# First two head projections of a hybrid backbone block: 128-column idle products, latent-token products of the second weight pair for both heads ahead of the context products, and the context squares' adds behind the latent tiles

## The chip, the cores and the metric

The program runs on one core of a Trainium2 chip. The metric is device time in microseconds (us) of one execution. The engines are PE (matrix products), DVE (vector), ACT (scalar), POOL and SP; nearly all loads are issued by SP's queue, in its program order. A block of 128 x 512 elements is written 128x512 here, 128 being the partitions.

## The reference

One layer of a generator block over 512 latent tokens and 256 context tokens, width D = 2048. Only its beginning matters here:

```python
mod = (c_act @ w_mod + b_mod)[:, None, :]            # c_act = silu(c)
mod_c = (cc_act @ w_mod + b_mod)[None, None, :]      # cc_act = silu(c_ctx)
sh1, sc1, gt1, sh2, sc2, gt2 = jnp.split(mod, 6, axis=-1)
...
h = rmsnorm(x, g_norm1) * (1 + sc1) + sh1            # latent tokens
hc = rmsnorm(ctx, g_norm1) * (1 + csc1) + csh1       # context tokens
lat_in, lat_gates = project_heads(h, w_in, ...)
ctx_in, ctx_gates = project_heads(hc, w_in, ...)
```

`rmsnorm` divides a token by the root of its mean square over the 2048 channels. `project_heads` multiplies by `w_in` (queries, keys and values of four GLA heads and four mLSTM heads). Scans over the tokens, an output projection and an MLP with a convolution follow; the change leaves them alone.

## The kernel before, in words

All matrix data are float32. A product of two float32 tiles is made of three products of parts: each operand is cut into a high part `hi` (a cast on ACT, line 110) and a low part `lo` (a subtraction on DVE, line 112), and `mm3` adds hi*hi, hi*lo and lo*hi (line 117 for all of them). A product written `fp32` (the modulation, the idle products, the sums of squares) goes through PE uncut and shows as two records in the trace.

The 2048 channels are 16 blocks of 128, taken as eight pairs `kp` = 0 to 7. `project_first` projects the first two heads, head 1 and head 0, pair by pair. A pair needs:

- Modulation. `mod_load(region, n)` loads four quarters (512 KB each) of the columns of `w_mod` for pair n; region 1 is the scale, region 0 the shift. `mod_rows` multiplies them by the activated c (tile `cact`) into the bank `ps_m`, and ACT copies the sums out (tile `rows_m`, line 299). `mod_cols` turns them into columns on PE (line 122), and DVE makes `scol` (scale) or `shcol` (shift) of them (lines 310 to 323).
- Tokens. `modulate` multiplies the latent block `xl` by `scol` and by the reciprocal root `rl` on DVE (line 808), and the context block `xc` by `scol` and `rc` (line 810). ACT then adds `shcol` and writes the high part (`hTh` for latent, `hch` for context, line 801), and DVE the low part (`hTl`, `hcl`, line 802).
- Weights. One 512 KB load `raw_h` for each head, cut into `hi_h` and `lo_h`.
- Products, in six groups g: queries and keys on latent tokens (0, 1), values on latent tokens (2, 3) and keys with values on context tokens (4, 5). Head 1's go through two turning PSUM banks (`early_group`, tile `a1`), and DVE adds each to a sum in SBUF (line 448, tile `e`). Head 0's add up in six banks of their own (`project_chunk`, tile `a0`). The trace calls both `a`.

Pair 0 is projected before any root is known, on tokens without root and shift (`bare`). Meanwhile `stream_rstd` squares the 16 latent blocks on ACT (line 770) and adds them on DVE (line 105, tile `sq_l`); one fp32 product with ones (`ss_l`) sums over partitions, and `mean_rsqrt` (lines 184 to 189) makes `rl`. The same is done for the eight context loads (`sq_c`, `ss_c`, `rc`). With a root known, pair 0's results are scaled after the fact: `scale_first` multiplies those with tokens in the free dimension by `rl` on DVE (line 102), `columns` makes columns `rcol` of the root (line 496, tile `diag`), and ACT scales the others by them (line 507). `shifted` adds the shift to `xl` for a later stage (line 823).

`idle(n)` issues n fp32 products on `cact` whose result nobody reads. `silu_rows` makes rows of the activated c, which POOL writes to DRAM (`crow_d`) and `last_rows` reads back spread over all partitions (two loads of 512 KB in SBUF), for the part of the modulation that DVE computes in later pairs.

What sets the order: within `project_first` every PE instruction is pinned to the order of the code (`tc.keep_in_program_order`). The other engines' orders are made by a scheduler, which puts work under `tc.high_priority()` first and obeys `tc.issue_after(ins)` (and `behind`, a list of them): an instruction is placed behind `ins` in the order, without a wait. At run time each engine goes through its list in order, and an instruction that waits for a semaphore holds up all behind it. A load waits for a free buffer: `raw_h` and every fourth modulation quarter share four (pool `wraw`), the other quarters seven (`mraw`).

Of the kernel before, what the change touches and what calls it, by code (L numbers as in the profile page):

```python
# [88 lines left out]
def block_kernel(ctx: ExitStack, tc: tile.TileContext, a: dict, out: bass.AP):  # L89
# [374 lines left out]
    def silu_rows():  # L464

        cr = [tmp.tile([2 * KT, P], F32, name=f"cr{i}", tag="rows") for i in range(2)]
        nc.sync.dma_start(cr[0], a["c_row"])
        S.activation(cr[1], cr[0], AF.Exp, scale=-1.0)
        V.tensor_scalar(out=cr[1], in0=cr[1], scalar1=1.0, scalar2=None, op0=ALU.add)
        V.reciprocal(out=cr[1], in_=cr[1])  # L470
        mul(cr[1], cr[0], cr[1])
        nc.gpsimd.dma_start(crow_d, cr[1])

    def idle(n):

        ps = psb("idle")
        for _ in range(n):
            mm(ps, flat(cact[:, 0:4, :]), flat(cact), start=True, stop=True)
# [20 lines left out]
    def scale_first(banks, sums, stream):  # L499
# [4 lines left out]
        for o in (sums, banks):  # L504
            for j in range(TJ) if stream == "x" else range(TJ, TJ + CJ):
                part = o[2 + j // 2][:, j % 2, :] if stream == "x" else o[j]
                S.activation(part, part, AF.Copy, scale=rcol[:, j : j + 1])
# [43 lines left out]
    def project_first():  # L551
# [12 lines left out]
        rows = mod_rows(1, 0, first_mod, lambda: idle(1))  # L564
        idle(1)
# [6 lines left out]
        idle(3)  # L572
# [5 lines left out]
        w1 = load_split(a["w_heads"][1, 1], "h1_1", by=OFF)  # L578
        for j in range(1, KT // 2):
            nc.sync.dma_start(xcp[j], a["ctxT"][j])  # L580
        w0_raw = load_raw(a["w_heads"][0, 1], "h0_1")
        stream_rstd(xl, rl, "l", T, bared)
        for g in range(2, 5):
            project_chunk(0, *w0, banks[g], g, 0, 1)
        rows = mod_rows(1, 1, raws[1])
        project_chunk(0, *w0, banks[5], 5, 0, 1)
        mod_cols(1, 1, *rows)
        rows = mod_rows(0, 1, raws[0])
        idle(1)
        mod_cols(0, 1, *rows)  # L590
        with tc.high_priority():
            modulate(1, "x")
            columns(range(TJ))
            scale_first(banks, sums, "x")
        for r in (1, 0):
            raws[r] = mod_load(r, 2)
        idle(3)
# [11 lines left out]
        for kp in range(1, KP):  # L609
            if kp == 1:  # L610
                silu_rows()
            for g in range(6):
                if g == 5 and 1 < kp < KP - 2:
                    rows = mod_rows(0, kp + 1, raws[0])
                if kp == 1 and g == 2:
                    with tc.high_priority():
                        stream_rstd([x.rearrange("p a b -> p (a b)") for x in xcp], rc, "c", TC)
                        modulate(1, "c")
                        columns(range(TJ, TJ + CJ))
                        scale_first(banks, sums, "c")  # L620
# [10 lines left out]
                if g == 2:  # L631
                    with tc.issue_after(ins):
                        if kp == 1:
                            with tc.high_priority():
                                w0 = split_new(w0_raw, "h0_1", (2, 512), by=OFF)
                        else:
                            w0 = load_split(a["w_heads"][0, kp], f"h0_{kp}", by=OFF)
# [4 lines left out]
                    if 1 < kp < KP - 3:  # L642
# [7 lines left out]
            if kp > 1 and kp + 1 < KP:  # L650
# [10 lines left out]
            for g in range(6):  # L661
                if g == 3 and 1 < kp < KP - 3:
                    rows = mod_rows(1, kp + 2, raws[1])
                if kp == 1 and g in (2, 4):
                    r = 2 - g // 2
                    rows = mod_rows(r, 2, raws[r])
# [18 lines left out]
                if g == 3 and 1 < kp < KP - 3:  # L685
# [1236 lines left out]
```

## Time and profile before

| what | value |
|---|---|
| median of 3 runs | 2393.97 us (2393.84 to 2395.94) |
| the profiled execution | 2394.47 us |
| its span in the trace | 2392.8 us |
| PE busy | 2360.2 us, 99% of the span |
| mean granted PE clock | 0.997 |
| first product of pair 0, of pair 1, of pair 2 | 18.48, 47.22, 78.19 us |

The profile is of one execution. Times on the timeline count from the start of the span. A timeline row gives the start, the duration, the engine, the line, the operation, output and inputs, the count of records merged, and in brackets the idle time of the engine before it and what ended that. Records of PE overlap: a 128x512 product that takes 0.39 us is followed by the next after 0.23 us.

### The profile page before, as it was taken

To read this page: it belongs to the slowest core of one execution; us is meant where nothing else is said; L and a number is where in the kernel's file an instruction comes from. 1 tells how busy PE (TensorE), PEld (TensorE's weight loads), DVE (VectorE), ACT (ScalarE), POOL (GpSimd) and SP (SyncE) were. 2 spreads that over 40 slices of the span, in tenths; PEclk is the share of its full clock that TensorE was granted. 3 is DMA by queue.
4 is the path that set the end of the run, shared out by engine and by line. 5 is a ranking of instruction groups with operands and counts; after the bars stand their busy time and mean duration, and the time that the engine had idled before them with its cause. 6 is when DMAs were issued, how large, how long until landed. Compare 5 with 4: busy or idle time off the path is not lost.

```text
span 2392.8 us, 38575 instructions
## 1 busy us (share of the span) xinstructions
PE 2360.2 (99%) x15310; PEld 2117.2 (88%) x15310; DVE 1811.7 (76%) x2924; ACT 1044.8 (44%) x1573; POOL 184.2 (8%) x236
## 2 busy tenths in 40 slices
PE   8999999999999999999999999999999999999998
PEld 4788899899998888888999999999999999999997
DVE  5777866654546676768998787878787878787886
ACT  5234543322233232327554444545454444444445
POOL 0000000000000000010011111111111111101022
PEclk9999999999999999999999999999999999999999
DMA  8871111234445879862374646464646464646464
GB/s 337 312 278 53 47 54 45 66 111 133 126 160 182 264 269 309 281 219 74 112 180 125 158 124 158 124 158 123 157 125 156 126 155 126 156 125 158 131 182 137
DMA packets 121703, 377.84 MB, mean 158 GB/s; under 512 B 14200, under 2 KB 15218, under 8 KB 121522
## 3 DMA queue, kind: packets, MB, share of 16 engines
q1 hardware_dynamic: 94066, 319.77, 40.7%
q0 software_dynamic: 27024, 54.82, 12.9%
q8 instruction: 120, 1.97, 0.3%
q10 hardware_dynamic: 432, 0.79, 0.1%
q14 instruction: 61, 0.50, 0.1%
HBM read 324.84 MB, written 50.48 MB: 157 GB/s over the span
## 4 chain that ended last, share of the span: by engine, by line
PE 93%; DVE 4%; ACT 2%; issue 1%; DMA 0%; DVEq 0%; ACTq 0%
PE dn L117 19%; PE uv L117 17%; PE ug L117 17%; PE a L117 17%; PE ga L117 7%; PE wo L117 7%; PE po L117 2%; PE ps_m L117 1%; PE sl L117 1%; PE st L117 1%; PE cst L117 1%; DVE ex L99 1%; PE idle L117 0%; DVE lo_h L112 0%; DVE e L448 0%
## 5 line engine op out<-in xcount | busy, mean ns | idle before, releaser
L117 PE MATMUL dn<-gh,hi_d 128*128 128x512 f32 x672 | 261.6, 389 | 0.0
L117 PE MATMUL dn<-gl,hi_d 128*128 128x512 f32 x672 | 261.5, 389 | 0.0
L117 PE MATMUL dn<-gh,lo_d 128*128 128x512 f32 x672 | 261.5, 389 | 0.0
L1639 DVE SCALAR_TENSOR_TENSOR cv<-pads,cwt,cv 128x512 f32<-128x512 f32 x344 | 240.8, 748 | 0.6
L1707 POOL DMA_DIRECT2D x2d<-st x160 | 139.6, 926 | 1096.3 <-ACT st L1706 1049.1
L112 DVE TENSOR_TENSOR lo_buv<-sum_uv,hi_buv 128x1024 fp32r<-128x1024 f32 x80 | 98.0, 1225 | 82.2 <-ACT hi_buv L110 80.2
L340 DVE SCALAR_TENSOR_TENSOR raw_m<-raw_m,crow 128x1024 f32<-128x1024 f32 x128 | 154.6, 1229 | 1.8 <-DMA raw_m<-in_w_mod 1.8
L117 PE MATMUL a<-hi_h,hTh 128*128 128x256 f32 x512 | 151.4, 296 | 1.4 <-ACT e L460 0.8
L117 PEld LDWEIGHTS dn<-gh,lo_d 128*128 128x128 f32 x672 | 126.1, 188 | 26.3
L117 PEld LDWEIGHTS dn<-gh,hi_d 128*128 128x128 f32 x672 | 126.1, 188 | 26.0 <-DVE u_ug L99 0.3
L117 PEld LDWEIGHTS dn<-gl,hi_d 128*128 128x128 f32 x672 | 126.1, 188 | 25.9
L117 PE MATMUL a<-lo_h,hTh 128*128 128x256 f32 x512 | 143.1, 279 | 0.0
L117 PE MATMUL a<-hi_h,hTl 128*128 128x256 f32 x512 | 142.9, 279 | 0.0
L112 DVE TENSOR_TENSOR lo_d<-raw_d,hi_d 128x1024 fp32r<-128x1024 f32 (+1 forms) x86 | 102.9, 1197 | 40.6 <-ACT hi_d L110 40.6
L110 ACT CAST hi_d<-raw_d 128x1024 fp32r<-128x1024 f32 (+1 forms) x86 | 88.7, 1032 | 101.8 <-PE dn L117 38.0
L117 PE MATMUL uv<-bqh,lo_auv 128*128 128x256 f32 x480 | 132.9, 277 | 0.0
L117 PE MATMUL uv<-bql,hi_auv 128*128 128x256 f32 x480 | 132.9, 277 | 0.0
L117 PE MATMUL ug<-bqh,lo_aug 128*128 128x256 f32 x480 | 132.8, 277 | 0.0
L117 PE MATMUL uv<-bqh,hi_auv 128*128 128x256 f32 x480 | 132.8, 277 | 0.0
L117 PE MATMUL ug<-bqh,hi_aug 128*128 128x256 f32 x480 | 132.8, 277 | 0.0
L117 PE MATMUL ug<-bql,hi_aug 128*128 128x256 f32 x480 | 132.8, 277 | 0.0
L117 PE MATMUL ug<-bth,hi_bug 128*128 128x256 f32 x480 | 132.6, 276 | 0.0
(482 smaller groups left out, 7282.4 us busy)
## 6 DMA issues: line engine op xcount, KB each, us to landing
raw_m<-in_w_mod SPq DMA_DIRECT2D x184, 512.0 KB, 5.3
raw_d<-in_w_down SPq DMA_DIRECT2D x82, 512.0 KB, 3.3
raw_ug<-in_w_up SPq DMA_DIRECT2D x80, 512.0 KB, 3.5
raw_uv<-in_w_up SPq DMA_DIRECT2D x80, 512.0 KB, 4.3
x2d<-st POOLq DMA_DIRECT2D x160, 256.0 KB, 5.4
raw_h<-in_w_heads SPq DMA_DIRECT2D x64, 512.0 KB, 3.6
raw_ga<-in_w_gates SPq DMA_DIRECT2D x32, 512.0 KB, 4.2
raw_wo<-in_w_out SPq DMA_DIRECT2D x32, 512.0 KB, 4.7
```

Of the source, the lines that this page charges most:

```text
L99: V.tensor_tensor(out=o, in0=x, in1=y, op=ALU.subtract)
L110: cast[0] = S.copy(hi, x).ins
L112: return V.tensor_tensor(out=lo, in0=x, in1=hi.bitcast(F32), op=ALU.subtract).ins
L117: ins = PE.matmul(*args, **kw)
L340: V.scalar_tensor_tensor(out=x, in0=x, scalar=1.0, in1=crow[0], op0=ALU.mult, op1=ALU.mult, accum_out=mtot[:, at : at + 1])
L1639: V.scalar_tensor_tensor(out=t3, in0=src, scalar=w, in1=t3, op0=ALU.mult, op1=ALU.add)
L1707: nc.gpsimd.dma_start(x2d[k], t, accum_op=ALU.add)
```

## The change

- `idle` multiplies 128 columns instead of 512, and there are 34 idle products instead of 15: 4 at the start as before, 2 instead of 1 between the quarters of the first modulation and around its columns, 8 instead of 3 ahead of pair 0, 2 at each of the columns of pair 1, and 10 instead of 3 ahead of pair 1.
- Pair 0 of head 0: its six groups all stand ahead of the latent root's product `ss_l`; before, groups 2 to 5 stood behind it.
- Pair 1 is taken out of the loop over `kp` and written out. On PE: groups 0 to 3 of head 1, groups 0 to 2 of head 0, then the context root `ss_c`, the scale's modulation of pair 2, group 3 of head 0, the shift's modulation of pair 2, then the context groups 4 and 5 of head 1 and of head 0. Before, `ss_c` stood behind group 1 of head 1, and each head's six groups stood together.
- `stream_rstd` of the context gets `(ins, ins)`: all its DVE adds, and its first two squares on ACT, are placed behind the last latent low part of pair 1 (`hTl`). `scale_first` gets two such lists: head 1's scaling stands behind the cast of its weights for pair 1, head 0's behind the cast of its own.
- Head 0's weights of pair 1 are cut right after pair 1's tokens are modulated. `silu_rows` (its tiles now under a tag of their own), `last_rows` and the load of the remaining constants move with the code, and so do the loads of later pairs in SP's queue. From pair 2 on the loop is as before, without its cases for pair 1; the counts of all real products are the same.

```diff
@@ -463,7 +463,7 @@
 
     def silu_rows():
 
-        cr = [tmp.tile([2 * KT, P], F32, name=f"cr{i}", tag="rows") for i in range(2)]
+        cr = [tmp.tile([2 * KT, P], F32, name=f"cr{i}", tag="cr") for i in range(2)]
         nc.sync.dma_start(cr[0], a["c_row"])
         S.activation(cr[1], cr[0], AF.Exp, scale=-1.0)
         V.tensor_scalar(out=cr[1], in0=cr[1], scalar1=1.0, scalar2=None, op0=ALU.add)
@@ -473,9 +473,9 @@
 
     def idle(n):
 
-        ps = psb("idle")
+        ps = psb("idle", (P, P))
         for _ in range(n):
-            mm(ps, flat(cact[:, 0:4, :]), flat(cact), start=True, stop=True)
+            mm(ps, flat(cact[:, 0:4, :]), flat(cact[:, 0:4, :]), start=True, stop=True)
 
     def bare(n, streams):
 
@@ -496,7 +496,7 @@
             V.scalar_tensor_tensor(out=junk, in0=rstd[:, P * j : P * j + P], scalar=1.0, in1=ident, op0=ALU.mult,
                                    op1=ALU.mult, accum_out=rcol[:, j : j + 1])
 
-    def scale_first(banks, sums, stream):
+    def scale_first(banks, sums, stream, queue=(), late=()):
 
         if stream == "x":
             for o in (*sums[0:2], *banks[0:2]):
@@ -504,7 +504,8 @@
         for o in (sums, banks):
             for j in range(TJ) if stream == "x" else range(TJ, TJ + CJ):
                 part = o[2 + j // 2][:, j % 2, :] if stream == "x" else o[j]
-                S.activation(part, part, AF.Copy, scale=rcol[:, j : j + 1])
+                with behind(late if o is banks else queue):
+                    S.activation(part, part, AF.Copy, scale=rcol[:, j : j + 1])
 
     first_bias = {}
 
@@ -561,40 +562,69 @@
         load_tokens(range(2, KT))
         raws = {r: mod_load(r, 1) for r in (1, 0)}
         idle(4)
-        rows = mod_rows(1, 0, first_mod, lambda: idle(1))
-        idle(1)
+        rows = mod_rows(1, 0, first_mod, lambda: idle(2))
+        idle(2)
         ins = mod_cols(1, 0, *rows)
         with tc.high_priority():
             w1 = split_new(w1_raw, "h1_0", (2, 512), by=OFF, after=(ins,))
             bared = bare(0, "x")
             w0 = split_new(w0_raw, "h0_0", (2, 512), by=OFF, after=bared[1:])
             bare(0, "c")
-        idle(3)
+        idle(8)
         early_pair(w1, sums)
         for g in range(2, 6):
             early_group(0, g, w1, sums)
         for g in range(2):
             project_chunk(0, *w0, banks[g], g, 0, 1)
         w1 = load_split(a["w_heads"][1, 1], "h1_1", by=OFF)
+        w1_cast = cast[0]
         for j in range(1, KT // 2):
             nc.sync.dma_start(xcp[j], a["ctxT"][j])
         w0_raw = load_raw(a["w_heads"][0, 1], "h0_1")
+        for g in range(2, 6):
+            project_chunk(0, *w0, banks[g], g, 0, 1)
         stream_rstd(xl, rl, "l", T, bared)
-        for g in range(2, 5):
-            project_chunk(0, *w0, banks[g], g, 0, 1)
         rows = mod_rows(1, 1, raws[1])
-        project_chunk(0, *w0, banks[5], 5, 0, 1)
+        idle(2)
         mod_cols(1, 1, *rows)
         rows = mod_rows(0, 1, raws[0])
-        idle(1)
+        idle(2)
         mod_cols(0, 1, *rows)
         with tc.high_priority():
-            modulate(1, "x")
+            ins = modulate(1, "x")
             columns(range(TJ))
-            scale_first(banks, sums, "x")
+            w0 = split_new(w0_raw, "h0_1", (2, 512), by=OFF)
+            scale_first(banks, sums, "x", (w1_cast,), (cast[0],))
+        silu_rows()
         for r in (1, 0):
             raws[r] = mod_load(r, 2)
-        idle(3)
+        idle(10)
+        for g in range(4):
+            early_group(1, g, w1, sums)
+        for g in range(3):
+            project_chunk(1, *w0, banks[g], g)
+        with tc.high_priority():
+            stream_rstd([x.rearrange("p a b -> p (a b)") for x in xcp], rc, "c", TC, (ins, ins))
+            modulate(1, "c")
+            columns(range(TJ, TJ + CJ))
+            scale_first(banks, sums, "c")
+        rows = mod_rows(1, 2, raws[1])
+        project_chunk(1, *w0, banks[3], 3)
+        mod_cols(1, 2, *rows)
+        rows = mod_rows(0, 2, raws[0])
+        early_group(1, 4, w1, sums)
+        mod_cols(0, 2, *rows)
+        ins = early_group(1, 5, w1, sums)
+        with tc.high_priority():
+            modulate(2, "xc")
+        w1 = load_split(a["w_heads"][1, 2], "h1_2", by=OFF)
+        raws[1] = mod_load(1, 3)
+        for g in range(4, 6):
+            project_chunk(1, *w0, banks[g], g)
+        with tc.issue_after(ins):
+            last_rows(0)
+            shifted(1)
+        nc.sync.dma_start(cst[:, 0:C_ID], a["consts"][:, 0:C_ID])
         loads = {(2, 0): (0, 1), (2, 1): (0, 0), (3, 0): (1, 1), (3, 1): (1, 0)}
         turns = {(2, 1): (0, 1), (3, 0): (0, 0), (4, 0): (1, 1), (4, 1): (1, 0)}
         lasts = {}
@@ -606,18 +636,10 @@
             if what == (1, 0) and g == 4:
                 last_end()
 
-        for kp in range(1, KP):
-            if kp == 1:
-                silu_rows()
+        for kp in range(2, KP):
             for g in range(6):
-                if g == 5 and 1 < kp < KP - 2:
+                if g == 5 and kp < KP - 2:
                     rows = mod_rows(0, kp + 1, raws[0])
-                if kp == 1 and g == 2:
-                    with tc.high_priority():
-                        stream_rstd([x.rearrange("p a b -> p (a b)") for x in xcp], rc, "c", TC)
-                        modulate(1, "c")
-                        columns(range(TJ, TJ + CJ))
-                        scale_first(banks, sums, "c")
                 if kp == 2 and g == 2:
                     rows = mod_rows(1, 3, raws[1])
...
@@ -659,30 +677,20 @@
                 with tc.issue_after(ins):
                     shift_first(1, sums)
             for g in range(6):
-                if g == 3 and 1 < kp < KP - 3:
+                if g == 3 and kp < KP - 3:
                     rows = mod_rows(1, kp + 2, raws[1])
-                if kp == 1 and g in (2, 4):
-                    r = 2 - g // 2
-                    rows = mod_rows(r, 2, raws[r])
                 if kp == KP - 3 and g == 1:
                     rows = mod_rows(0, 0, raws[2])
                 project_chunk(kp, *w0, banks[g], g)
                 with tc.issue_after(ins):
                     last_step(kp, 1, g)
-                if kp == 1 and g in (2, 4):
-                    mod_cols(2 - g // 2, 2, *rows)
                 if g == 2 and kp + 1 < KP:
                     w1 = load_split(a["w_heads"][1, kp + 1], f"h1_{kp + 1}", by=OFF)
-                    if kp == 1:
-                        raws[1] = mod_load(1, 3)
-                        with tc.issue_after(ins):
-                            last_rows(0)
-                        nc.sync.dma_start(cst[:, 0:C_ID], a["consts"][:, 0:C_ID])
-                    elif kp + 2 < KP - 1:
+                    if kp + 2 < KP - 1:
                         raws[0] = mod_load(0, kp + 2)
                     if (kp, 1) in loads:
                         lasts[loads[kp, 1]] = last_load(*loads[kp, 1])
-                if g == 3 and 1 < kp < KP - 3:
+                if g == 3 and kp < KP - 3:
                     mod_cols(1, kp + 2, *rows)
                 if kp == KP - 3 and g == 2:
...
```

Around the latent root, PE's order. `a_1_171` to `a_5_175` are head 0's banks of groups 1 to 5 (the last number is a buffer's), `ps_m_1` is the modulation of pair 1. Before:

```order
L117 MATMUL a_1_171<-hTh_259,lo_h_0_264 128x512
L117 MATMUL ss_l<-sq_l,cst 128x512
L117 MATMUL a_2_172<-hi_h_0_263,hTh_255 128x256
...
L117 MATMUL a_2_172<-hi_h_0_263,hTl_260 128x256
...
L117 MATMUL a_4_174<-hi_h_0_263,hch_267 128x384
...
L117 MATMUL a_4_174<-hi_h_0_263,hcl_272 128x384
L117 MATMUL ps_m_1_457<-raw_m_1_0_198,cact 32x256 x4
...
L117 MATMUL a_5_175<-hi_h_0_263,hch_267 128x384
...
L122 MATMUL ps_m_1_457<-cst,rows_m_1_474 128x128 x2
```

After:

```order
L117 MATMUL a_1_171<-hTh_263,lo_h_0_268 128x512
L117 MATMUL a_2_172<-hi_h_0_267,hTh_259 128x256
...
L117 MATMUL a_3_173<-hi_h_0_267,hTh_259 128x256
...
L117 MATMUL a_4_174<-hi_h_0_267,hch_271 128x384
...
L117 MATMUL a_5_175<-hi_h_0_267,hcl_276 128x384
L117 MATMUL ss_l<-sq_l,cst 128x512
L117 MATMUL ps_m_1_472<-raw_m_1_0_198,cact 32x256 x4
...
L117 MATMUL idle<-cact 128x128 x2
L122 MATMUL ps_m_1_472<-cst,rows_m_1_489 128x128 x2
```

Groups 2 to 5 of head 0 stand ahead of `ss_l`, and nothing but idle products stands between the modulation's sums and its columns.

Around the context root, PE's order. `a_1_0` to `a_1_5` are head 1's groups of pair 1, `ss_c` the context squares' sum, `ps_m_2` the modulation of pair 2, `a_2_0` pair 2's first group. Before:

```order
L117 MATMUL a_1_0_570<-hTh_514,hi_h_1_357 128x512
...
L117 MATMUL a_1_1_578<-hTh_514,hi_h_1_357 128x512
...
L117 MATMUL ss_c<-sq_c,cst 128x256 x2
L117 MATMUL a_1_2_638<-hi_h_1_357,hTh_514 128x256
...
L117 MATMUL a_1_4_670<-hi_h_1_357,hch_622 128x384
...
L117 MATMUL a_0_170<-hTh_514,hi_h_1_652 128x512
...
L117 MATMUL ps_m_2_700<-raw_m_2_0_542,cact 32x256 x4
...
L117 MATMUL a_3_173<-hi_h_1_652,hTh_514 128x256
...
L117 MATMUL ps_m_2_766<-raw_m_2_0_550,cact 32x256 x4
...
L117 MATMUL a_5_175<-hi_h_1_652,hch_622 128x384
...
L117 MATMUL a_2_0_821<-hTh_805,hi_h_2_738 128x512
```

After:

```order
L117 MATMUL a_1_0_594<-hTh_527,hi_h_1_366 128x512
...
L117 MATMUL a_1_1_602<-hTh_527,hi_h_1_366 128x512
...
L117 MATMUL a_1_3_624<-hi_h_1_366,hTh_527 128x256
...
L117 MATMUL a_0_170<-hTh_527,hi_h_1_543 128x512
...
L117 MATMUL a_2_172<-hi_h_1_543,hTh_527 128x256
...
L117 MATMUL ss_c<-sq_c,cst 128x256 x2
L117 MATMUL ps_m_2_714<-raw_m_2_0_567,cact 32x256 x4
...
L117 MATMUL a_3_173<-hi_h_1_543,hTh_527 128x256
...
L117 MATMUL ps_m_2_750<-raw_m_2_0_575,cact 32x256 x4
...
L117 MATMUL a_1_4_769<-hi_h_1_366,hch_698 128x384
...
L117 MATMUL a_1_5_781<-hi_h_1_366,hch_698 128x384
...
L117 MATMUL a_2_0_841<-hTh_793,hi_h_2_811 128x512
```

`ss_c` moved behind five more groups, and the context groups moved behind both modulations of pair 2.

Between the latent root and pair 1, DVE's order. `rstd` is the root, `e_0`, `e_1`, `a_0_170` and `a_1_171` the results of pair 0 that are multiplied by it, `xl_130` and `xl_131` pair 1's latent blocks. Before:

```order
L189 SCALAR_TENSOR_TENSOR rstd<-scr_l,rstd 128x512
L102 TENSOR_TENSOR e_0_293<-e_0_293,rstd 128x512
L102 TENSOR_TENSOR e_1_295<-e_1_295,rstd 128x512
L102 TENSOR_TENSOR a_0_170<-a_0_170,rstd 128x512
...
L310 TENSOR_REDUCE scol<-ps_m_1_457 128x4
...
L808 SCALAR_TENSOR_TENSOR xl_130<-xl_130,scol,rstd 128x512
...
L496 SCALAR_TENSOR_TENSOR diag_528,rcol<-rstd,cst 128x128
L310 TENSOR_REDUCE shcol<-ps_m_1_487 128x4
...
L112 TENSOR_TENSOR lo_h_1_358<-raw_h_1_355,hi_h_1_357 128x1024
L105 TENSOR_TENSOR sq_c<-sq_c,sq_c_588 128x512
L802 SCALAR_TENSOR_TENSOR hTl_515<-xl_130,shcol,hTh_514 128x512
...
L802 SCALAR_TENSOR_TENSOR hTl_519<-xl_131,shcol,hTh_518 128x512
```

After:

```order
L189 SCALAR_TENSOR_TENSOR rstd<-scr_l,rstd 128x512
L310 TENSOR_REDUCE scol<-ps_m_1_472 128x4
L102 TENSOR_TENSOR e_0_302<-e_0_302,rstd 128x512
...
L813 SCALAR_TENSOR_TENSOR xl_130<-xl_130,scol,rstd 128x512
L813 SCALAR_TENSOR_TENSOR xl_131<-xl_131,scol,rstd 128x512
L102 TENSOR_TENSOR e_1_304<-e_1_304,rstd 128x512
...
L496 SCALAR_TENSOR_TENSOR diag_535,rcol<-rstd,cst 128x128
...
L310 TENSOR_REDUCE shcol<-ps_m_1_499 128x4
L496 SCALAR_TENSOR_TENSOR diag_541,rcol<-rstd,cst 128x128
...
L112 TENSOR_TENSOR lo_h_1_367<-raw_h_1_364,hi_h_1_366 128x1024
L807 SCALAR_TENSOR_TENSOR hTl_528<-xl_130,shcol,hTh_527 128x512
L807 SCALAR_TENSOR_TENSOR hTl_532<-xl_131,shcol,hTh_531 128x512
```

Three of the four multiplications by the root, and three of the four `diag` rows, still stand ahead of the shift's reduction (`shcol`); the context squares' adds (`sq_c`) left the stretch between `lo_h` and the second `hTl`.

More of the change, by code (lines that the diff above doesn't have):

```diff
@@ L632, in project_first @@
                     with tc.issue_after(ins):
-                        if kp == 1:
[L634 to L637, printed above, removed]
+                        w0 = load_split(a["w_heads"][0, kp], f"h0_{kp}", by=OFF)
                     if kp == 2:
@@ L641, in project_first @@
                         lasts[loads[kp, 0]] = last_load(*loads[kp, 0])
-                    if 1 < kp < KP - 3:
+                    if kp < KP - 3:
                         raws[1] = mod_load(1, kp + 2)
@@ L649, in project_first @@
                         first_w = {h: load_raw(a["w_heads"][h, 0], f"b{h}") for h in (1, 0)}
-            if kp > 1 and kp + 1 < KP:
+            if kp + 1 < KP:
                 if kp + 1 < KP - 1:
@@ L671, in project_first @@
                     last_step(kp, 1, g)
-                if kp == 1 and g in (2, 4):
-                    mod_cols(2 - g // 2, 2, *rows)
                 if g == 2 and kp + 1 < KP:
                     w1 = load_split(a["w_heads"][1, kp + 1], f"h1_{kp + 1}", by=OFF)
-                    if kp == 1:
-                        raws[1] = mod_load(1, 3)
-                        with tc.issue_after(ins):
-                            last_rows(0)
-                        nc.sync.dma_start(cst[:, 0:C_ID], a["consts"][:, 0:C_ID])
-                    elif kp + 2 < KP - 1:
+                    if kp + 2 < KP - 1:
                         raws[0] = mod_load(0, kp + 2)
@@ L693, in project_first @@
                     first_shifts(first_w)
-            if kp == 1:
-                with tc.high_priority():
-                    ins = modulate(2, "xc")
         return banks, sums
```

## The prediction

> **What bounds the kernel now.** I read the busy times first, then PE's waits up to 110 us, then windows, and then the timeline around each wait.
>
> ```profile
> PE 2360.2 (99%) x15310; PEld 2117.2 (88%) x15310; DVE 1811.7 (76%) x2924; ACT 1044.8 (44%) x1573; POOL 184.2 (8%) x236
> PE ss_c L117 <- DVE sq_c L105: 3.5, 1, 3.5
> PE ss_l L117 <- DVE sq_l L105: 2.5, 1, 2.5
> PE a L117 <- ACT hch L801: 2.1, 1, 2.1
> PE a L117 <- DVE hTl L802: 1.8, 4, 0.9
> PE a L117 <- ACT hTh L801: 0.7, 2, 0.4
> core 0: us, PE busy (x) PEld busy (x) DVE busy (x) ACT busy (x) POOL busy (x), PEclk, DMA share, GB/s
> 18.50:33.30 14.80, 11.52 (x62) 9.19 (x60) 13.34 (x20) 12.69 (x25) 0.00 (x0) 1.00 1.04 415
> 55.40:63.00 7.60, 5.50 (x28) 5.03 (x28) 4.92 (x10) 1.42 (x4) 0.00 (x0) 0.78 0.10 18
> 105.00:200.00 95.00, 93.71 (x721) 77.90 (x723) 75.10 (x141) 33.98 (x54) 6.28 (x11) 1.00 0.70 242
> ```
>
> PE is the bound of the whole (99%), and from 105 to 200 us it is busy 93.71 of 95 us. So what brings PE's first real products forward should arrive almost whole at the end: all counts of real products stay, and PE's order from pair 2 on is the old one. A wait row reads: total us, times, longest. The waits to 110 us are where something can be won. The window 55.40 to 63.00 adds a second loss: behind the 3.5 us wait for `ss_c` PE worked at a mean clock of 0.78, which is (1 - 0.78) x 7.6 = 1.7 us.
>
> **The way I sum.** I follow five points of PE's list: pair 0's first product, `ss_l`, pair 1's first product, pair 2's first product, and pair 2's own waits. The gain at the last point is the gain of the kernel.
>
> **Idle products and pair 0.** A long form of `idle` holds up the modulation's columns and the first real product, although their data have long been there:
>
> ```profile
> 3.77 5.87 PE L117 MATMUL idle<-cact 128*128 128x512 f32 x8 [3.77 <-DVE cact L102]
> 9.57 0.64 PE L117 MATMUL ps_m<-raw_m,cact 128*32 128x256 f32 x8
> 10.14 1.12 PE L117 MATMUL idle<-cact 128*128 128x512 f32 x2
> 11.36 1.05 ACT L110 CAST hi_h<-raw_h 128x1024 fp32r<-128x1024 f32 x1 [8.54 <-DMA raw_h<-in_w_heads]
> 15.15 0.37 ACT L299 COPY rows_m<-ps_m 128x256 f32<-128x256 f32 x1 [2.75 <-PE ps_m L117]
> 17.00 1.33 ACT L487 ACTIVATE hTh<-xl,scol 128x512 fp32r<-128x512 f32 x2 [1.48 <-DVE scol L320]
> 18.48 1.58 PE L117 MATMUL a<-hTh,hi_h 128*128 128x512 f32 x4
> ```
>
> From 9.57 on PE turns in a circle of 1.62 us: a quarter of the modulation (0.57 to the next start) and one idle product (1.06; two records are one product). At 128 of 512 columns I estimate an idle product at 0.27 (a quarter of 1.06) to 0.53 us (half, if something in it does not shrink with the columns); two of them cost 0.5 to 1.1. What then ends the wait are the loads. `raw_h` stands in SP's queue directly behind the four quarters, and ACT could cast it at 11.36; at 415 GB/s 512 KB take 1.26 us, so the last quarter has landed by about 10.1. Its products take 0.6, so the sums end at 10.7 and ACT's copy starts. From that copy to `hTh` took 17.00 - 15.15 = 1.85: 12.5. ACT's cast, 11.36 to 12.41, lies in between and may push it by some tenths. First product at `hTh`'s first half, 0.7 later: 13.2 to 13.8, and the eight idle products ahead of it (some 2 us from 11.5) end about there. I take 13.4: **5.1 us** earlier.
>
> On the clock. The first eight records took 5.87 us, 0.73 each, against 0.53 each in the pair at 10.14: PE starts slow, and lost 8 x 0.2 = 1.6 us there. The new idle products leave PE gaps between 5 and 10 us, while it waits for quarters. The Trainium skill, page "TensorE: Matmul & The Clock Gate", section "Why this matters for your kernels", asks for at least 4 us of continuous work to reach full speed; here the trace agrees as far as that start shows it (1.6 us lost in 5.87). If gaps denied the full clock until pair 0, this would cost the sum what I price among the rivals; I don't count it, since the window 18.50 to 33.30 kept 1.00 with PE busy 11.52 of 14.8 us.
>
> **To `ss_l`.**
>
> ```profile
> 21.45 11.84 DVE L105 TENSOR_TENSOR sq_l<-sq_l,sq_l 128x512 f32<-128x512 f32 x15
> 30.44 0.39 PE L117 MATMUL a<-hTh,lo_h 128*128 128x512 f32 x1
> 33.35 1.13 PE L117 MATMUL ss_l<-sq_l,cst 128*128 128x512 f32 x2 [2.52 <-DVE sq_l L105]
> 33.91 0.69 PE L117 MATMUL a<-hi_h,hTh 128*128 128x256 f32 x1
> 38.19 1.93 PE L117 MATMUL ps_m<-raw_m,cact 128*32 128x256 f32 x32
> 40.05 0.44 PE L117 MATMUL a<-hi_h,hch 128*128 128x384 f32 x1
> 41.20 0.38 PE L122 MATMUL ps_m<-cst,rows_m 128*128 128x128 f32 x2
> ```
>
> The work from pair 0's first product to the end of head 0's group 1 took 30.67 - 18.48 = 12.2. Groups 2 to 5 of head 0, which now stand ahead of `ss_l`, took 33.91 to 38.19 and 40.05 to 41.20, 5.4 with their start-up, and I take 5.1 back to back. So `ss_l` is reached at 13.4 + 12.2 + 5.1 = 30.7. The squares' adds ended at 33.3; they began behind the low parts, which come 5.1 us earlier, but need the last latent loads, which SP sends no sooner: I place their end between 28.2 (all of the 5.1) and 30.5. So the 2.52 us wait goes; its cover is the 5.1 us of moved products, and without it 2.5 would be left. `ss_l` itself moves from 33.35 to 30.7: of the 5.1 won, 2.6 is left here, and 5.4 of work that stood behind now stands ahead.
>
> **To pair 1.**
>
> ```profile
> 37.87 0.69 DVE L189 SCALAR_TENSOR_TENSOR rstd<-scr_l,rstd 128x512 f32<-128x512 f32 x1
> 38.60 1.29 DVE L102 TENSOR_TENSOR e<-e,rstd 128x512 f32<-128x512 f32 x2
> 42.53 1.41 DVE L808 SCALAR_TENSOR_TENSOR xl<-xl,scol,rstd 128x512 f32<-128x512 f32 x2
> 43.85 0.29 DVE L496 SCALAR_TENSOR_TENSOR diag<-rstd,cst 128x128 f32<-128x128 f32 x1
> 46.46 0.71 ACT L801 ACTIVATE hTh<-xl,shcol 128x512 fp32r<-128x512 f32 x1
> 47.22 0.50 PE L117 MATMUL a<-hTh,hi_h 128*128 128x512 f32 x1
> ```
>
> Now DVE sets the start. From `ss_l` to the root's end took 38.56 - 33.35 = 5.2: 35.9. Then DVE's list: `scol` 0.6, four multiplications by the root 2.5 (0.64 each), two `xl` 1.35, four `diag` 1.3 (0.33 each), `shcol` 0.35: 6.1, to 42.0. Then `hTh` and the start of PE, 47.22 - 46.46 = 0.76: pair 1 starts at **42.8**, 4.4 us earlier. PE's work between (two modulations of 1.9, their columns, four short idle products and ten more, about 8.5 us from 30.7) ends near 39.3, so a new wait of some 3.5 us stands here. The tokens and weights of this pair must have landed; ahead of 47.22 nothing in the waits above points at a load.
>
> **Pair 1 to pair 2.**
>
> ```profile
> 55.47 1.63 PE L117 MATMUL ss_c<-sq_c,cst 128*128 128x256 f32 x4 [3.49 <-DVE sq_c L105]
> 63.04 0.45 PE L117 MATMUL a<-hi_h,hch 128*128 128x384 f32 x1 [2.07 <-ACT hch L801]
> 78.19 0.50 PE L117 MATMUL a<-hTh,hi_h 128*128 128x512 f32 x1 [0.24 <-ACT hTh L801]
> 78.98 0.50 PE L117 MATMUL a<-hTl,hi_h 128*128 128x512 f32 x1 [0.29 <-DVE hTl L802]
> ```
>
> This stretch took 78.19 - 47.22 = 31.0. In it lie 3.49 + 2.07 + 0.24, the two `hTl` waits inside (1.8 in all, less 0.29 twice behind pair 2's start: 1.2), and 1.7 of lost clock: 8.7. Work: 22.3.
> New losses, worked out:
> - `hTl` at pair 1: DVE still has `lo_h` (1.2, as the `lo_h` row among the loads below) ahead of the first `hTl`. As before: 1.0, between 0.5 and 1.5.
> - Clock: the new 3.5 us wait ahead of pair 1 is as long as the 3.49 that was followed by 0.78, and longer than the 2.52 that kept 1.00. I charge 1.7, between 0 and 1.7. The skill's same section warns of gaps above about 3 us; by that line the charge stands, and by a wait cut just under it the sum would be 1.7 lower. The rows bracket the limit between 2.52 and 3.49.
> - Head 0's `lo_h` stands on DVE behind four `sq_c` adds and three sums `e`, and is needed after groups 0 to 3 (8.3 us, as 18.48 to 27.9 less its waits): 0.6, between 0 and 1.5.
> - The context chain: from `ss_c` to the first `hch` product took 63.04 - 55.47 = 7.6, slow clock and DVE's queue included. Its cover is now the scale's modulation 1.9, group 3 1.4, the shift's modulation 1.9 and columns: 5.3. So 0 (a chain free of `lo_h`, 1.2, and of 0.8 of slow `ss_c` fits) to 2.3; I take 0.5.
> - `ss_c` itself: groups 0 to 3 and 0 to 2 are some 15 us of work, against 8 adds of 0.65 on DVE: no wait, and its 3.49 goes.
>
> Sum 3.8, so the stretch takes 26.1 and pair 2 starts at 42.8 + 26.1 = 68.9, **9.3 us** earlier.
>
> **Pair 2's own waits and the queues.** Pair 2's tokens now stand behind head 1's group 5 with head 0's context groups as cover, 2 x 1.05 us and more, so the 0.24 is counted, and of 0.29 + 0.44 + 0.29 behind it I take 0.9 as gone: **10.2** in all.
>
> ```profile
> 47.70 14.14 SPq L284 DMA_DIRECT2D raw_m<-in_w_mod  x2
> 60.23 1.22 DVE L112 TENSOR_TENSOR lo_h<-raw_h,hi_h 128x1024 fp32r<-128x1024 f32 x1
> 67.74 1.09 POOL L354 DMA_DIRECT2D rows<-crow_d  x2 [1.44 <-DMA crow_d<-cr]
> ```
>
> SP's queue stood from 47.70 until that `lo_h` gave its buffer free. Head 0's cut now comes near 51, so the held quarter and all behind it (constants, pair 2's later weights) go out about 10 us sooner. `silu_rows`, its 16 KB load and POOL's two spread loads (1 MB, 2.5 us at 415 GB/s) come about 10 us sooner too, and meet pair 2's loads. I cost this at nothing: loads of pair 2 then have 6 us and more until their use.
>
> **The sum.** 2394.47 - 10.2 = 2384.3 against the profiled execution, which lies 0.50 above the median 2393.97; so 2383.8 against the median, and with tenths in favour where I took the later end (13.4, 0.6 for `lo_h`) I say 2383.6.
>
> **Rivals.**
> - *Cold clock at pair 0.* Gaps among the first quarters put off the full clock, and PE loses the 1.6 us of its first records once more in pair 0's: 2385.2. For it: the slow start above. Against: 11.52 of 14.8 kept 1.00. Chance 0.12.
> - *The new losses stay out.* No clock loss and half of the rest: 2381. For it: the bracket 2.52 to 3.49. Chance 0.10.
> - *The lead is swallowed.* DMA ran at 415 GB/s to beyond 33 us; if pair 1's weights or last modulation quarter are not there before 45 to 47, most of the first 4.4 stays away and pair 2's loads shift with it: 2389 to 2394. Against: no wait of PE to 110 us names a DMA. Chance 0.10.
> - *Slower.* DVE's adds `sq_c` are now last in a filled list; PE stands at `ss_c`, and behind it stand the modulations whose buffers SP needs for pair 3, so loads miss too. It decides once the adds end more than 13 us behind their rows: PE would reach `ss_c` at about 58, so at about 71. The price is the delay beyond it: an end at 74 gives 2394 + 3 = 2397. Against: 8 adds of 0.65 and what is between them, about 10 us from 45. Chance 0.02.
>
> **How the numbers follow.** The forecast case has 0.66: 2383.6, on its own 2380.5 to 2387. The range 2379.5 to 2388.5 takes in the first two rivals and leaves the last two and tails out. A measurement here tells about 0.2%, 4.8 us, from no change; below 2389.2 lie the forecast, the first two rivals and part of the third. Faster 0.88, same 0.10, slower 0.02.
>
> **What would show it.** After: pair 0's first product near 13.4; no wait at `ss_l`, near 30.7; a wait of 2.5 to 4.5 us ahead of pair 1 near 42.8, with `hTh` as its end and a clock below 1 in one window behind it; no wait of 3 us at `ss_c`; the first `hch` product with a wait under 2.3; pair 2 near 69. Wrong it would be if a DMA shows among PE's waits, if `sq_l` still holds `ss_l`, or if the lead at pair 2 is given back before 200 us.

## The result and the profile after

The changed kernel takes 2381.10 us (median of 4 executions, 2380.13 to 2382.72), the kernel before 2394.07 beside it: a ratio of 0.9945, 95% interval [0.9928, 0.9962]. That is 13.0 us less; I had forecast 2383.6 (10.5 less) in a range of 2379.5 to 2388.5. The profiled execution, 2382.72, is the slowest of the four; its span is 2381.0 us, 11.8 less than before. One later execution of the changed kernel (in *again*, below) took 3372.14 us at a mean clock of 0.654 and is left out of every comparison.

PE's waits up to 100 us, after (total us, times, longest):

```profile
PE idle L117 <- DVE cact L102: 3.8, 1, 3.8
PE a L117 <- ACT hTh L806: 2.3, 1, 2.3
PE a L117 <- DVE lo_h L112: 0.9, 2, 0.5
PE ps_m L122 <- ACT rows_m L299: 0.6, 1, 0.6
PE a L117 <- ACT e L460: 0.6, 1, 0.6
PE a L117 <- DVE e_c L448: 0.5, 1, 0.5
```

The waits for `sq_l`, `sq_c` and `hch` are gone. What came is one wait for `hTh` and several of half a microsecond. The timeline at the points of the sum, after:

```profile
13.75 1.26 PE L117 MATMUL a<-hTh,hi_h 128*128 128x512 f32 x4
30.25 1.02 PE L117 MATMUL ss_l<-sq_l,cst 128*128 128x512 f32 x2
41.63 0.79 PE L117 MATMUL a<-hTh,hi_h 128*128 128x512 f32 x1 [2.29 <-ACT hTh L806]
42.67 0.80 PE L117 MATMUL a<-hTl,hi_h 128*128 128x512 f32 x1 [0.25 <-DVE hTl L807]
55.44 1.02 PE L117 MATMUL ss_c<-sq_c,cst 128*128 128x256 f32 x4
64.86 0.44 PE L117 MATMUL a<-hi_h,hch 128*128 128x384 f32 x1 [0.51 <-DVE e_c L448]
68.11 0.40 PE L117 MATMUL a<-hTh,hi_h 128*128 128x512 f32 x1
```

Pair 0 starts 4.7 us earlier, pair 1 5.6, pair 2 10.1. `ss_c` stands at the same time as before, 55.44 against 55.47; but seven groups of pair 1 are done by then instead of two. The rows from 41.63 on last 0.79 where a 128x512 product elsewhere lasts 0.39: PE is slow there. The windows show it (columns as before; PEclk is the third from the end):

```profile
38.06:41.47 3.41, 1.28 (x12) 1.09 (x10) 3.34 (x14) 0.83 (x2) 0.00 (x0) 1.00 1.04 369
41.47:44.88 3.41, 3.00 (x6) 2.11 (x7) 2.50 (x4) 3.41 (x9) 0.00 (x0) 0.50 1.02 411
44.89:48.30 3.41, 3.41 (x11) 2.74 (x10) 1.81 (x3) 2.73 (x4) 0.00 (x0) 0.50 1.03 420
```

Two windows at half clock, 6.83 us, are up to 3.4 us of lost clock; in time they cost some 2 us (*idle20* below). To compare kernels behind the projection I use the first product `glr`, which stands at the same place of PE's list in all of them. Before, then after:

```profile
203.33 1.10 PE L117 MATMUL glr<-gm,cst 128*96 128x512 f32 x2
```

```profile
192.73 1.10 PE L117 MATMUL glr<-gm,cst 128*96 128x512 f32 x2
```

The lead there is 10.6 us. The rest of the span's 11.8 comes up near 1079 us, where PE was slow before and was slow for half as long after. These two windows are of before, then of after:

```profile
1076.50:1083.40 6.90, 6.90 (x26) 5.98 (x24) 1.41 (x2) 1.65 (x4) 0.00 (x0) 0.51 0.38 140
```

```profile
1065.50:1068.90 3.40, 3.40 (x13) 2.85 (x11) 0.37 (x3) 0.00 (x0) 0.00 (x0) 0.50 0.97 372
```

3.4 us less at half clock is 1.7 us. That stretch is no part of the change, and it was slow in 6 of the 14 traces of this study, so the lead at `glr` is the measure of the change. In the 13 traces beside that of before, which was itself slow there for two windows, the lead at the end of the span is that at `glr` plus 0 to 3.4 us.

### The profile page after: what moved, and what is told of

The parts are those of the page before. It is cut to its first block, busy times and chain, and to the rows that moved or that the text cites. A ratio compares the mean times of both kernels' runs of the same rounds, so it can differ in the third digit from the quotient of the medians.

```text
span 2381.0 us, 38657 instructions
## 1 busy us (share of the span) xinstructions
PE 2354.7 (99%) x15348; PEld 2119.9 (89%) x15348; DVE 1810.4 (76%) x2924; ACT 1045.6 (44%) x1573; POOL 184.4 (8%) x236
## 4 chain that ended last, share of the span: by engine, by line
PE 92%; DVE 4%; DMA 2%; ACT 1%; issue 1%; SPq 0%; DVEq 0%; ACTq 0%
PE dn L117 19%; PE uv L117 17%; PE ug L117 17%; PE a L117 16%; PE ga L117 7%; PE wo L117 7%; PE po L117 2%; DMA raw_h<-in_w_heads 1%; PE sl L117 1%; PE st L117 1%; DMA raw_m<-in_w_mod 1%; PE cst L117 1%; PE ps_m L117 1%; DVE ex L99 1%; DVE lo_h L112 0%
## 5 line engine op out<-in xcount | busy, mean ns | idle before, releaser
L117 PEld LDWEIGHTS dn<-gh,lo_d 128*128 128x128 f32 x672 | 126.1, 188 | 26.1
```

Source lines behind the costliest of these rows:

```text
L117: ins = PE.matmul(*args, **kw)
```

## The experiments

Each kernel was timed in 5 executions (*idle_only* and *head_by_head* in 11) beside the kernel before. The times and intervals are of these; everything else is of one trace each. "Lead" is 203.33 less the start of `glr` in the kernel's trace, "ss_c" the start of that product, pair 0 and 1 the starts of their first product.

| kernel | median us | before beside it | ratio, 95% interval | pair 0 | pair 1 | ss_c | lead |
|---|---|---|---|---|---|---|---|
| idle_only | 2394.62 | 2394.39 | 0.9998 [0.9989, 1.0007] | 13.90 | 46.50 | 55.81 | -0.3 |
| order_only | 2383.21 | 2394.60 | 0.9955 [0.9943, 0.9968] | 18.37 | 46.79 | 57.94 | 7.9 |
| old_idle | 2384.08 | 2394.39 | 0.9958 [0.9946, 0.9971] | 18.81 | 46.40 | 58.38 | 7.4 |
| early_root | 2382.80 | 2394.39 | 0.9949 [0.9936, 0.9963] | 15.39 | 45.86 | 57.38 | 8.7 |
| head_by_head | 2392.32 | 2394.39 | 0.9992 [0.9983, 1.0001] | 15.27 | 43.16 | 54.08 | 0.1 |
| again (the changed kernel) | 2381.85 | 2393.88 | 0.9952 [0.9940, 0.9965] | 14.41 | 42.30 | 55.48 | 10.2 |
| free_adds | 2382.95 | 2393.88 | 0.9956 [0.9944, 0.9968] | 15.99 | 43.87 | 58.26 | 7.9 |
| idle20 | 2382.83 | 2393.88 | 0.9957 [0.9945, 0.9969] | 14.52 | 42.40 | 54.40 | 10.2 |
| scale_late | 2381.65 | 2393.88 | 0.9952 [0.9940, 0.9964] | 13.73 | 39.02 | 56.95 | 9.1 |
| warm_start | 2383.29 | 2394.60 | 0.9951 [0.9938, 0.9963] | 14.55 | 42.49 | 54.24 | 10.2 |
| warm20 | 2385.45 | 2394.60 | 0.9959 [0.9947, 0.9972] | 14.99 | 42.88 | 54.90 | 10.3 |
| scale_mid | 2379.60 | 2394.60 | 0.9939 [0.9926, 0.9953] | 14.66 | 39.94 | 53.94 | 11.9 |

**Which part brings the time.** *again* repeats the changed kernel: 12.0 us less than before beside it, a wait of 2.35 ahead of pair 1 and one slow window behind it. *idle_only* is the kernel before with the new idle products and counts (without the two ahead of the scale's columns of pair 1, where a real group stands).

```diff
-        ps = psb("idle")
+        ps = psb("idle", (P, P))
-            mm(ps, flat(cact[:, 0:4, :]), flat(cact), start=True, stop=True)
+            mm(ps, flat(cact[:, 0:4, :]), flat(cact[:, 0:4, :]), start=True, stop=True)
...
```

> The kernel before, with the idle products alone changed (128 columns, the new counts). Theory 1 (leads on PE add up until a chain on DVE cuts them): pair 0's first product at 13.75 instead of 18.48, but the squares' adds end at 29.5 as after the change, so the wait at ss_l grows from 2.5 to about 4 us, ss_l at 29.6, and 3.7 us of 4.7 stay; pair 1 near 43.5; 2390.3 us. Theory 2 (loads set the context root): ss_c stays near 55.5 and the lead is given back there: 2393 to 2394 us.

Measured: no gain that can be told from the spread. Theory 1 fell. The timeline:

```profile
29.70 2.08 PE L117 MATMUL ss_l<-sq_l,cst 128*128 128x512 f32 x2 [3.98 <-DVE sq_l L105]
46.50 0.51 PE L117 MATMUL a<-hTh,hi_h 128*128 128x512 f32 x1 [0.73 <-ACT hTh L801]
55.81 1.91 PE L117 MATMUL ss_c<-sq_c,cst 128*128 128x256 f32 x4 [2.97 <-DVE sq_c L105]
63.40 0.45 PE L117 MATMUL a<-hi_h,hch 128*128 128x384 f32 x1 [2.04 <-ACT hch L801]
```

The 4.6 us of pair 0 are 3.6 at `ss_l`, whose wait grew to 3.98 as expected. In and behind that wait PE ran at half clock (28.70 to 35.50, window row at 0.50), and of the lead 0.7 is left at pair 1. At `ss_c` it is nothing: DVE's adds end at 55.75, against 55.41 before. Theory 2 has the place right and not the reason: no square of ACT waits for a load there. The last three adds stand in DVE's list behind a sum `e` that waited 1.19 for PE at 52.87.

*head_by_head*: the changed kernel with pair 1 in the old way on PE.

```diff
-        for g in range(4):
+        for g in range(2):
             early_group(1, g, w1, sums)
-        for g in range(3):
-            project_chunk(1, *w0, banks[g], g)
...
+        for g in range(2, 6):
+            ins = early_group(1, g, w1, sums)
+        for g in range(3):
+            project_chunk(1, *w0, banks[g], g)
...
```

> The changed kernel, with pair 1's groups head by head and ss_c behind head 1's group 1, DVE's and the other orders kept as far as the scheduler keeps them. Theory 1: a wait of 3 to 5 us at ss_c and one of about 2 at the first hch product come back, with slow clock behind: 2386 to 2388 us. Theory 2 (adds and loads set the end of pair 1 whatever PE does meanwhile): less than 1.5 us lost, 2382.5 us.

Measured: 2392.32, which can't be told from the kernel before (2.1 us less, with an interval that reaches no change), and 4 us more than the dearer of the two expectations. Pair 1 starts 4.1 us earlier than before, and all of it is gone at `glr`:

```profile
43.16 0.49 PE L117 MATMUL a<-hTh,hi_h 128*128 128x512 f32 x1 [2.35 <-ACT hTh L806]
54.08 2.07 PE L117 MATMUL ss_c<-sq_c,cst 128*128 128x256 f32 x4 [5.51 <-DVE sq_c L105]
60.16 0.44 PE L117 MATMUL a<-hi_h,hch 128*128 128x384 f32 x1 [0.34 <-ACT hch L806]
75.46 0.51 PE L117 MATMUL a<-hTh,hi_h 128*128 128x512 f32 x1 [0.24 <-ACT hTh L806]
```

```profile
78.46:81.87 3.41, 3.41 (x12) 2.17 (x15) 0.82 (x3) 0.00 (x0) 0.00 (x0) 0.50 0.59 239
```

The wait at `ss_c` is longer than before (5.51 for 3.49), and `ss_c` takes 2.07 (1.63 before, 1.02 in the changed kernel): slow clock again. Of the 4.1 us, 1.4 are left at `ss_c` and 2.7 at pair 2 (75.46). So not all of it is lost at `ss_c`: up to 1.7 of the rest goes in a slow window behind pair 2's start, which the trace of before doesn't have. Since this kernel keeps the placed adds, the early cut and the moved loads, these bring nothing that can be told without PE's new order.

*order_only*: the changed kernel with the old idle products and with `ss_l` behind group 1 as before, so that only pair 1 (its order, the placed adds, the early cut and the moved loads) is new.

```diff
+        stream_rstd(xl, rl, "l", T, bared)
-        for g in range(2, 6):
+        for g in range(2, 5):
             project_chunk(0, *w0, banks[g], g, 0, 1)
-        stream_rstd(xl, rl, "l", T, bared)
         rows = mod_rows(1, 1, raws[1])
-        idle(2)
+        project_chunk(0, *w0, banks[5], 5, 0, 1)
...
```

> The kernel before with the new pair 1 alone: old idle products, and ss_l behind head 0's group 1 as before; the order of pair 1, the placed adds, the early cut of head 0's weights and the moved loads are as in the changed kernel. Theory 1 (the cover of ss_c and of the context chain carries the gain, since DVE's adds end near 55 whatever PE does): the lead of old_idle less the little that ss_l is worth: pair 2's lead 6.5 to 7.5, 2386 to 2387.5 us. Rival (the three parts add up and each is needed): about 2389 to 2390 us.

Measured: 2383.21, most of the gain by itself, with a lead of 7.9 of 10.6 at `glr`; at pair 2 it is 7.6, where theory 1 said 6.5 to 7.5. At the end it is more than either theory said; its trace has no slow stretch near 1079 us, which may be the reason. Its window across pair 1, to be read beside the 30.97 us that this stretch took before:

```profile
46.79:70.57 23.78, 21.98 (x170) 17.34 (x169) 19.84 (x43) 15.92 (x33) 1.77 (x3) 1.00 0.66 251
```

```profile
57.94 1.02 PE L117 MATMUL ss_c<-sq_c,cst 128*128 128x256 f32 x4
67.34 0.45 PE L117 MATMUL a<-hi_h,hch 128*128 128x384 f32 x1 [0.51 <-DVE e_c L448]
```

The same products run in 23.78 instead of 30.97 us, at full clock. Pair 1 starts only 0.4 us earlier. So the cover of the context chain carries most of the change, and the earlier start the rest, 2.3 to 2.7 us at `glr` (against *again* and against the result). Whether the order would bring as much without the early cut and the placed adds, no run shows.

*old_idle* and *early_root* take one part out of the changed kernel: the first has the old `idle` and its counts (the diff of *idle_only* turned round, and none ahead of the scale's columns of pair 1), the second has the diff shown for *order_only*.

> The changed kernel, with the old idle products (512 columns, old counts). Theory 1: everything up to pair 1 moves back by the 4.7 us of pair 0: pair 0 at 18.5, ss_l at 35.0 without a wait, pair 1 at 46.3, 2385.8 us. Theory 2 (DVE's adds and the loads have slack that takes part of it up): pair 1 moves by 2 to 3 only, 2383.5 us.

> The changed kernel, with ss_l back behind head 0's group 1 and group 5 and the columns as before. Theory 1: PE comes to ss_l near 25.4, waits 4 us, ss_l at 29.6; groups 2 to 5 (5.1 us) then fill PE while DVE makes the root, so that the wait ahead of pair 1 and its slow clock are gone and PE's own work starts pair 1 near 43.8: 2380.5 to 2382.5 us, about the same. Theory 2 (the move of ss_l is a gain of its own, the 2.5 us of its wait): 2383.6 us.

Both lie between. Without the short idle products pair 1 starts 4.8 us later and 3.2 of lead are lost at `glr`. Theory 1 is right on pair 1 (46.40 for 46.3), theory 2 on the time: part of the loss is taken up behind it. Without the move of `ss_l` 1.9 is lost, but pair 0 started 1.6 later in that trace for another reason (below). If all of that came through, the move is worth 0.3 us; and *order_only*, with `ss_l` in its old place, has 0.5 more lead than *old_idle*. So nothing shows a gain of its own for this move, as theory 1 said. PE waited 3.96 at `ss_l` and then not ahead of pair 1: the wait changed its place.

*free_adds*: the context squares and their adds are not placed.

```diff
-            stream_rstd([x.rearrange("p a b -> p (a b)") for x in xcp], rc, "c", TC, (ins, ins))
+            stream_rstd([x.rearrange("p a b -> p (a b)") for x in xcp], rc, "c", TC)
```

> The changed kernel without the placement of the context squares' adds and squares behind pair 1's low parts. Theory 1: two adds of 0.65 us stand again ahead of the low parts on DVE, PE waits about 0.7 us more at hTl and nothing is won at ss_c, where there was no wait: 2381.8 us. Rival (the placement is what frees pair 1): 2383 us or more.

Inconclusive. The wait at the first `hTl` grew from 0.54 (*again*) to 0.85, at `ss_c` there was none, as theory 1 said; but this trace also started pair 0 1.6 us later, and was slow for two windows instead of one. What the placement is worth alone is not told apart from that.

**The new wait and the clock.** *idle20*:

```diff
-        idle(10)
+        idle(20)
```

> The changed kernel with 20 instead of 10 idle products ahead of pair 1. Clock theory: the wait of 2.3 us shrinks to under 0.3, pair 1 starts at 41.6 to 41.9, the clock stays full behind it, 1.7 to 3.4 us less: 2378 to 2379.5 us. Rival (the slow clock has another cause, or PE's rate there is not what ends the stretch): 2381 us.

The wait of 2.3 and the slow windows behind it are gone, as the clock theory says. Pair 2's lead is 1.0 us better than in *again*. From pair 1's start to pair 2's it took 26.48 us with two slow windows (the result), 25.84 with one (*again*) and 24.70 with none. So two windows cost some 1.8 us and not 3.4; without them PE waits 0.59 for DVE's `e` (47.04). But the time is not better. By 203 us the lead is 10.2, that of *again*. Its waits from 100 to 150 us:

```profile
PE ps_m L117 <- DMA raw_m<-in_w_mod: 0.7, 2, 0.5
PE ps_m L122 <- ACT rows_m L299: 0.4, 1, 0.4
```

Waits for a modulation load stand where *again* had none. So loads take back 0.7 of the 1.0; this is the rival of the swallowed lead, at a later place and a smaller price than I gave it.

*warm_start*, and *warm20*, which has both diffs:

```diff
-        idle(4)
-        rows = mod_rows(1, 0, first_mod, lambda: idle(2))
+        idle(6)
+        rows = mod_rows(1, 0, first_mod, lambda: idle(3))
```

> The changed kernel with 6 instead of 4 idle products at the start and 3 instead of 2 between the first quarters, so that PE has no pause there. Start theory (the pauses for the first loads put off the full clock in some executions, and cost 0.7 to 2.2 us of pair 0's start): the full clock comes by 8.8 us, pair 0 starts at 13.7 to 14.3, the times spread less, and the median is 0.5 to 1 us lower than the changed kernel's: 2380.5 to 2381.3 us. Rival (the longer row of idle products costs as much as it saves): 2382 us.

> As warm_start, with 20 idle products ahead of pair 1. Theory 1: no slow clock behind pair 1's start either, the lead at pair 2 grows by 1.5 to 3 us, and where loads do not take it back the end is 2378.5 to 2379.5 us. Rival (the loads of pairs 3 and 4 cap the lead near 10.6 us by 200 us, as in idle20): 2380.5 to 2381.5 us with PE's waits for raw_m or later low parts grown by what was won.

The full clock came by 7.8 and 8.7 us, as the start theory says, and pair 0 still started at 14.55 and 14.99: the longer row costs what it saves. For *warm_start* that is the rival, and its time is 1.3 us above even that. A weight load takes lead back there: ACT's cast waits for `raw_h` until 137.67, and PE 1.72 behind it, at 140.63. For *warm20* neither expectation holds: 2385.45 is 4 us above the rival's. The trace is of its fastest execution (2383.30) and has the lead of the others at `glr`, so what the slower ones lost is not shown.

*scale_late* puts pair 0's scalings behind pair 1's low parts:

```diff
             ins = modulate(1, "x")
-            columns(range(TJ))
+            with tc.issue_after(ins):
+                columns(range(TJ))
             w0 = split_new(w0_raw, "h0_1", (2, 512), by=OFF)
-            scale_first(banks, sums, "x", (w1_cast,), (cast[0],))
+            with tc.issue_after(ins):
+                scale_first(banks, sums, "x", (w1_cast,), (cast[0],))
```

*scale_mid* is *warm_start* with that, and a written order: the sums' scalings first, then the context adds, and the banks' scalings behind the sums' (in `scale_first` the multiplications by `rl` are left out, since they stand here):

```diff
             ins = modulate(1, "x")
-            columns(range(TJ))
+            with tc.issue_after(ins):
+                columns(range(TJ))
+                muls = [mul(o, o, rl) for o in sums[0:2]]
             w0 = split_new(w0_raw, "h0_1", (2, 512), by=OFF)
-            scale_first(banks, sums, "x", (w1_cast,), (cast[0],))
+            with tc.issue_after(muls[1]):
+                for o in banks[0:2]:
+                    mul(o, o, rl)
+            scale_first(banks, sums, "x", (w1_cast, ins), (cast[0],))
...
-            stream_rstd([x.rearrange("p a b -> p (a b)") for x in xcp], rc, "c", TC, (ins, ins))
+            stream_rstd([x.rearrange("p a b -> p (a b)") for x in xcp], rc, "c", TC, (ins, muls[1]))
```

> The changed kernel with pair 0's scalings (columns and multiplications by the latent root) placed behind pair 1's low parts. If DVE's list between root and shift sets pair 1's start: 2.5 to 3 us of that list leave, pair 1 starts at 39.3 behind the idle products, without a wait and at full clock: 2376 to 2379 us. Rival (pair 2's loads or head 0's lo_h then hold PE up): 2380 to 2381 us, with a wait of PE for a DMA or lo_h after 50 us.

> As warm_start, and pair 0's scalings behind pair 1's low parts, the rows diag and the multiplications of the two sums e first, the context adds behind them, the multiplications of the two banks last. If only the order of the scalings made scale_late wait for e: pair 1 starts at 39.3 to 40 without a wait of over 0.5 us, the wait for e of 3.0 is gone, ss_c is then set by DVE's adds at 54 to 55 (1 to 2 us of wait), and the end is 2379 to 2380.5 us. Rival (what is won at pair 1 is given back at ss_c and at the loads): 2381 to 2382 us.

In *scale_late* pair 1 starts 2.6 us earlier, at 39.02, and then waits 2.95 for `e` (four context adds stood ahead of its scaling) and runs two windows slow. *scale_mid* mends this:

```profile
PE a L117 <- DVE lo_h L112: 2.1, 1, 2.1
PE a L117 <- DVE e L448: 1.1, 2, 0.6
```

Pair 1 starts at 39.94, the wait for `e` is 0.6, and a wait of 2.1 for head 0's `lo_h` takes most of what was won; `ss_c` has no wait. Its lead of 11.9 is the largest, so the loads set no fixed cap near 10.6, which the rival of *warm20* supposed; and 2379.60 is the lowest median. Its interval overlaps that of the changed kernel, so it is better by the traces, and only likely so by the times.

## Why the prediction was right, and where its steps were wrong

- *Pair 0*: 13.75 for 13.4. In other executions the rival of the cold clock came true in part, to which I had given 0.12: PE lost the time in the first modulation, ahead of pair 0, and not in pair 0's products. Here *free_adds*, in which the quarters' products last 1.08 until 11.7 us and 0.64 from 12.8 on, when the full clock came (7.34 in the trace of the result):

```profile
6.34 1.08 PE L117 MATMUL ps_m<-raw_m,cact 128*32 128x256 f32 x8 [0.54 <-DMA raw_m<-in_w_mod]
10.67 1.08 PE L117 MATMUL ps_m<-raw_m,cact 128*32 128x256 f32 x8
12.84 0.64 PE L117 MATMUL ps_m<-raw_m,cact 128*32 128x256 f32 x8
```

  The idle products no longer bridge the wait for the first load (0.54), and with the short ones pair 0 starts anywhere from 13.7 to 16.0. The price is up to 2.2 us, 0.6 more than I gave it.
- *`ss_l`*: 30.25 for 30.7, without a wait; the adds ended at 29.51, inside my bounds.
- *Pair 1*: 41.63 for 42.8. DVE's list took a little less than its rows said (5.5 for 6.1), so `hTh` came earlier than I thought and the wait was 2.29, just under the 2.5 to 4.5 that I had named.
- *Clock*: charged 1.7 and bracketed by a wait of 2.52 and one of 3.49; behind a wait of 2.29 two windows ran at half clock, and cost 1.8 to 2.1 us (26.48 from pair 1 to pair 2, for 24.70 in *idle20* and 24.41 in *warm_start*, which have none). So the charge was about right and its ground wrong: length alone doesn't decide, since the wait of 2.29 lost the clock and that of 2.52 kept it. The Trainium skill's line ("TensorE: Matmul & The Clock Gate", "Why this matters for your kernels") of gaps above about 3 us fails here in the same way.
- *Pair 1 to pair 2*: 26.5 us for 26.1: a little more for the clock, less at `hTl` (0.25 for 1.0) and `lo_h` (0.39 for 0.6), more in the context chain (0.63 at `rows_m` and 0.51 at `e_c` for 0.5, and none for `hch`). That these errors nearly cancel is luck. I also counted 8 adds for the context squares; there are 7.
- *Lead behind pair 2*: 10.6 for 10.2. The rest of the 13.0 (12.0 in *again*) is the stretch near 1079 us and the spread of executions, which no step of mine held.

The five points came out right. The step that failed is the premise ahead of them, that what brings PE's first real products forward arrives almost whole at the end. *idle_only* brings them 4.6 us forward and gains nothing: 3.9 of it is gone at pair 1, by a longer wait at `ss_l` and the slow clock behind it, and the rest at `ss_c`. In *head_by_head* pair 1 itself starts 4.1 us earlier without the new order, and nothing of that is left at `glr`. *order_only* has 7.9 with pair 1 only 0.4 earlier. So the 4.4 us that I booked on the earlier start and the 4.9 on the stretch behind it can't be had one by one: the new order alone brings 7.9, and the earlier start 2.3 to 2.7 on top of it and nothing that shows without it. DVE's adds for `ss_c` ended between 52.5 and 57.9 us in all 14 traces, whether pair 1 started at 39.0 or at 47.2; an early PE waits there unless it has other work. What sets the end of these adds was not taken apart.

## What to carry to other kernels

A term of a sum is won only if the next join does not wait for another engine: follow a lead to that join before it is booked, and ask what cover stands there. Moving independent work between a chain and the product that waits for it brought 8 us; bringing the same work forward by 4 to 5 us brought nothing that could be told from the spread. Where an engine is filled with idle work to hold its clock, the filling must bridge the waits, not merely shorten the row; but in *warm_start* the longer row that did so cost what it saved.

## What the runs showed of the hardware that I had not expected

In each trace the changes of PE's clock lie on a fixed grid of 3.41 us windows, and up to 70 us PE's busy share of one window tells the clock of the next. Before, the wait of 2.52 at `ss_l` fell across two windows, and 2.93 of the 3.49 at `ss_c` fell into one:

```profile
28.65:32.06 3.41, 2.18 (x10) 1.46 (x8) 2.99 (x5) 2.55 (x5) 0.00 (x0) 1.00 1.02 417
32.06:35.47 3.41, 2.12 (x12) 1.65 (x13) 1.13 (x2) 0.96 (x2) 0.00 (x0) 1.00 1.03 411
52.54:55.95 3.41, 0.48 (x2) 0.46 (x3) 2.15 (x4) 2.85 (x5) 0.00 (x0) 1.00 0.09 34
55.95:59.37 3.42, 3.42 (x15) 3.17 (x15) 1.64 (x4) 0.89 (x2) 0.00 (x0) 0.50 0.00 0
```

Shares of 0.64 and 0.62 kept the clock, 0.14 lost it. After, 0.37 lost it (38.06 to 41.47 above), and the next window, 0.88 busy, did not win it back; the one after it, 1.00 busy, did. In *warm_start* the same wait, 2.35 long, lay across two windows, and no slow one followed:

```profile
38.49:41.90 3.41, 1.65 (x15) 1.46 (x14) 3.34 (x15) 0.55 (x2) 0.00 (x0) 1.00 1.03 410
41.90:45.32 3.42, 2.28 (x8) 1.44 (x9) 3.07 (x5) 3.42 (x8) 0.00 (x0) 1.00 1.03 420
```

Up to 70 us in the 14 traces, every window at full clock with a share of 0.44 or less was followed by a slow one, and none of 0.47 or more was. Behind that it is less clean: at 75 us in *head_by_head* a window of 0.63 lost the clock. The stretch near 1079 us doesn't fit by busy time either: the window ahead of each slow one there has a share of 0.72, as have windows there that kept the clock. What decides in those two places is open.
